# Seven-product projections joined to the feed-forward stage before them: combinations formed in its last down-projection, all three value projections as doubles by way of DRAM

## The chip, the core and the metric

The kernel runs on one core of a Trainium2 chip. The metric is device time of one execution in microseconds (us). The core has five engines that run at the same time, each in its own fixed order of instructions: TensorE (PE, matrix products), VectorE (DVE), ScalarE (ACT), GpSimd (POOL) and SyncE (SP), which only issues transfers here. Transfers (DMAs) go through queues: q1 holds those that SP issues, q0 those that POOL issues.

## What is computed

One encoder layer for 512 tokens of 1024 channels, in float32:

```
x = x + 1/2 * SwiGLU_1(RMSNorm(x))          # 1024 -> 2816 -> 1024
h = RMSNorm(x)
A, B, gates = h @ w_in                      # 4608 + 1536 + 2048 columns
  A: 3 groups of 8 heads of 64, dilated windows (128,1) (512,4) (2048,16), relative bias,
     groups combined by their softmax denominators
  B: grouped-query attention, 8 heads of 128, 2 key/value heads, normed and rotated q, k
mix = (sigmoid(gA) * (oA @ P_A) + sigmoid(gB) * (oB @ P_B)) @ w_out
x = x + mix
x = x + 1/2 * SwiGLU_2(RMSNorm(x))
y = RMSNorm(x)
```

The change lies in the projections of branch A: its q and k (24 blocks of 128 columns) and its three values V0, V1, V2 (512 columns each, one for each group).

## The kernel before

**Products.** x is held transposed, as eight tiles of 128 channels by 512 tokens. Every float32 product is made of three matmuls of rounded operands (`mm3`, L249 to L252): each operand is split into a high part H (a cast on ACT) and a rest L (a subtraction on DVE). The normed input is `hH`, `hL` (`norm_h`, L389 and L390), without the factor 1/rms of each token, which is applied to the results: `r` holds it by token in partitions, `R` by token in columns, `acc` first the sum of squares (`norm_sq`, L400, on POOL for all but the last two tiles) and later `R` in the order of residues mod 4. Weights come as tiles of 128x1024 in rings of buffers (`wr`, `wa`, `ws`, `wt`) and are split the same way (`wh` L235, `wl` L236).

**Doubles.** In parts of the kernel two blocks of 128 columns are computed together from seven half-size products instead of eight (`strassen`). Its steps are A11, S1, S2, A12, S3, S4 and A22; each is 24 matmuls of 256 columns. They need combinations of the quarters of the input (`Traw`, split into `TQ`), combinations of the weights (formed by an adding transfer on POOL, L217, and a DVE addition, L234), and additions of the results (`evict`). For the mixer this is done in `project_qk` for ten q/k pairs (f = 0, 2, ..., 8) and for V0 (f = 10). The q/k results go through `qo` to DRAM (`qk_d`, L744) and come back for attention (`fetch`, L682).

**The stages around the joint.** `ffn` ends the first feed-forward stage with its last down-projection: eight rows of matmuls, whose results are added to x (`down`, `add`, L521 and L522) and turned into hH and hL. Then the pools of the stage close. `project_qk` opens its own, and starts with a stream of plain projections: V1 token by token (`token`), then gates 0 to 3 (`feat`). While these run, the statistics r and R are made (`stat_r` L414, `stat_R` L422, `stat_p` L431), and `tq_steps` makes the combinations (L697 to L706). Then come the doubles. V1 and V0 stay in SBUF. V2 is a plain token projection too, the first item of the fill after the doubles.

**Attention A and fill.** After the doubles, `fetch` brings q and k. The remaining plain projections are fill: a generator whose groups of three matmuls (one item of `feat` is eight groups) are put between the parts of attention. First come `GAP_F` = 16 groups, then for each pair of heads `hp` scores (`scores_a`: S L831, bias tiles W by SP L804 and L805, exponentials, an exchange of maxima and sums by way of DRAM L852 to L859) and values (`values_a`: transposes T, copies PT L902, products with V L882). After the first scores, `until(fill, ("v", 2))` runs the fill until V2 is complete.

**What sets the order.** PE runs in the order in which the program is written (`manual_schedule`). On the other engines a scheduler decides the order when the kernel is built. Transfers of one queue start in that order.

Of the kernel before, what the change touches and what calls it, by code (L numbers as in the profile page):

```python
# [11 lines left out]
F32 = mybir.dt.float32  # L12
# [11 lines left out]
NSQ = 10  # L24
STEPS = ("A11", "S1", "S2", "A12", "S3", "S4", "A22")
GAP_F = 16
# [44 lines left out]
class Layer:  # L71
    def __init__(self, ctx, tc, a):
# [26 lines left out]
        self.qk_d = self.dram.tile([2 * NSQ, 128, T], F32, name="qk_d")  # L99
        gates = lambda lo, hi: [("g", j) for j in range(lo, hi)]  # L100
# [3 lines left out]
        span = {"v": ("wav", 4), "qk": ("waq", 2), "g": ("wg", 1), "b": ("wb", 4), "pa": ("wpa", 4)}  # L104
        self.order = self.ffn_order("a")
        for kind, n in self.items:
            if kind == "sw":
                self.order += [("swq", at) for at in self.slots(range(0, NSQ + 2, 2))]
# [18 lines left out]
    @staticmethod  # L127
    def slots(fs):
        at = {7 * i + 2 * j: (f, step) for i, f in enumerate(fs) for j, step in enumerate(STEPS)}
        return [at[k] for k in sorted(at)]  # L130
# [58 lines left out]
    def load(self, n):  # L189
# [17 lines left out]
        def part(q):  # L207
            if name[2] == "q" and f == NSQ:
                return self.a["wav0"][2 * int(q[1]) + int(q[2]) - 3].rearrange("p (a c) -> p a c", a=2)
            i, c = 2 * f + int(q[1]) - 1, 512 * (int(q[2]) - 1)  # L210
            return w[i:i + 3:2, :, c:c + 512].rearrange("a p c -> p a c")
# [90 lines left out]
    def strassen(self, s, fs, evict):  # L302
        st, order = {}, self.slots(fs)
        end = self.used + len(order) - 1
        for f, step in order:
# [7 lines left out]
            for j in range(2):  # L313
                for k in range(4):
                    ops = self.right(step, k)
                    if s == "q" and f == NSQ:
# [7 lines left out]
    def right(self, step, k):  # L324
# [4 lines left out]
        if self.TQ:  # L329
            c = {"S1": 0, "S3": 1, "A22": 2, "S2": 3}[step]  # L330
            return tuple(t[:, k, c, :] for t in self.TQ)
        c = {"S1": 0, "A22": 1, "S2": 2}[step]
        return self.TH[:, c, k, :], self.TL[:, c, k, :]

    def t_steps(self, g, gp):
# [4 lines left out]
        def put(d):  # L340
            if d == 0:
                both.extend(gp.tile([128, 2048], F32, tag=f"g{2 + c}", name=f"T{c}") for c in range(2))
                raw.extend(both[c // 2][:, 1024 * (c % 2):1024 * (c % 2) + 1024] for c in range(4))
            nc.scalar.activation(both[d // 4].rearrange("p (a c) -> p a c", a=2)[:, :, 256 * (d % 4):256 * (d % 4) + 256],
# [47 lines left out]
    def norm_sq(self, d, pool=NK - 2):  # L392
# [3 lines left out]
        else:  # L396
            sq = self.tmp.tile([128, T], F32, tag="t", name="sq")
            nc.scalar.activation(sq, self.x[d], AF.Square)
            eng = nc.vector if d >= pool else nc.gpsimd
# [26 lines left out]
    def stat_p(self):  # L426
        nc = self.nc
        nc.vector.tensor_copy(self.acc.rearrange("p (r m) -> p r m", r=4), self.R.rearrange("p (m r) -> p r m", r=4))
        pr = self.aux("rps")
        for r in range(4):  # L430
            nc.tensor.transpose(pr[:, r:r + 1], self.acc[0:1, 128 * r:128 * r + 128], self.ident[0:1, 0:1])  # L431
        nc.vector.tensor_copy(self.r[:, 4:8], pr[:, 0:4])

    def ffn(self, s, gin, gnext, hooks, out=None, side=None):
        with ExitStack() as ctx:
# [6 lines left out]
            self.ffn_run(s, gin, gnext, hooks, out, side or {}, pool("g", bufs=1))  # L442
            self.wx = None

    def ffn_run(self, s, gin, gnext, hooks, out, side, gp):
        nc = self.nc
        g, t, c, half = [], {}, {}, []

        def new():
            both = gp.tile([128, 2048], F32R, tag=f"g{len(g) // 2}", name="gg")  # L450
            return both[:, :1024], both[:, 1024:]
# [93 lines left out]
        for gi, hi in enumerate(ends):  # L545
            last = hi == NF
# [10 lines left out]
            rows = [(list(g), lambda ps, d=d: done(d, ps)) for d in range(NK)]  # L557
# [71 lines left out]
    def stream(self, items):  # L629
        nc = self.nc  # L630
        for kind, n in items:
            if kind == "v":
                toks = [(lambda t, r=r: t[:, r:T:4]) if n else (lambda t, r=r: t[:, 128 * r:128 * r + 128]) for r in range(4)]

                def done(j, b, g=n):
                    rc = self.r[:, j + (4 if g else 0):j + (5 if g else 1)]
                    if j % 2:
                        nc.vector.tensor_scalar(self.V[g][:, j, :], b, rc, None, op0=ALU.mult)
                    else:
                        nc.scalar.activation(self.V[g][:, j, :], b, AF.Copy, scale=rc)  # L640

                yield from self.token("wav", 4 * n, toks, done)
            elif kind == "qk":
# [10 lines left out]
            elif kind == "g":  # L654
# [6 lines left out]
                yield from self.feat("wg", n, done)  # L661
# [22 lines left out]
    def tq_steps(self, cp):  # L684
        nc = self.nc
        raw = {}

        def put(k):
            raw[k] = cp.tile([128, 4, 256], F32, tag="c1", name="Traw")
            for e in range(2):  # L690
                d = k + 4 * e
                nc.scalar.activation(raw[k][:, 2 * e:2 * e + 2], self.x[d].rearrange("p (a n) -> p a n", a=2), AF.Copy,
                                     scale=self.par[:, G_MIX + d:G_MIX + d + 1])

        def sums(k):
            b = [raw[k][:, c] for c in range(4)]
# [6 lines left out]
        def part(k):  # L703
            H, L = (t[:, k] for t in self.TQ)
            nc.scalar.copy(H, raw[k])
            nc.vector.tensor_sub(L, raw[k], f32(H))  # L706

        return [lambda fn=fn, k=k: fn(k) for k in range(4) for fn in (put, sums, part)]

    def project_qk(self):  # L710
        nc, tc = self.nc, self.tc
        with ExitStack() as ctx:
            pool = lambda n, **k: ctx.enter_context(tc.tile_pool(name=n, reuse_waits="tile", **k))
            tp = self.shifted(pool("qT", bufs=1), 64)
            self.TQ = [tp.tile([128, 4, 4, 256], F32R, name=f"TQ{c}") for c in "HL"]
            self.wx = self.shifted(pool("wxq", bufs=1), 64)
            cp, qp = pool("cq", bufs=2), pool("qo", bufs=2)
            steps = self.tq_steps(cp)
            hooks = {7: self.stat_r, 12: self.stat_R, 17: self.stat_p}
            for n, _ in enumerate(self.stream(self.items[:self.head])):  # L720
                if n in hooks:
                    hooks[n]()
                if n > 8 and n % 4 == 0 and steps:
                    steps.pop(0)()
            assert not steps
            c = {}
# [19 lines left out]
            def tokens(src, half, cols, neg):  # L746
                for j in range(2):
                    i = 2 * half + j
                    out, part, rc = self.V[0][:, i, cols], src[:, 256 * j:256 * j + 256], self.r[:, i:i + 1]
                    if neg:  # L750
                        nc.vector.tensor_scalar(out, part, rc, -1.0, op0=ALU.mult, op1=ALU.mult)
                    else:
                        nc.scalar.activation(out, part, AF.Copy, scale=rc)

            def evict(f, step, ps):
# [15 lines left out]
                elif step == "S4":  # L771
                    nc.vector.tensor_add(hi, ps, hi)
                    if f == NSQ:
                        tokens(lo, 0, slice(0, 256), False)
                        tokens(hi, 1, slice(0, 256), False)
                        return
                    o = qp.tile([128, 1024], F32, tag="qo", name="qo")
# [3 lines left out]
                elif f == NSQ:  # L781
# [484 lines left out]
```

## Time and profile before

| | us |
|---|---|
| median of 3 runs | 1260.6 (1260.19 to 1260.75) |
| the profiled execution | 1261.44 |
| its span | 1259.7 |
| ACT busy | 595.7 |
| POOL busy | 120.9 |
| last down-projection of the first stage | 314.82 to 347.49 |
| V1, then gates 0 to 3 | 347.49 to 372.29 to 394.07 |
| doubles of the mixer | 394.07 to 509.29 |
| first scores | 520.86 |

Times inside the kernel are microseconds from the start of the span. Instructions appear with the line of the kernel, their output and input names (`mm`: a PSUM bank, `gg`: the activations of the feed-forward stage) and their shape.

### The profile page before, as it was taken

The page shows a single profiled execution, that of the slowest core. Times are in us where ns is not written, and L with a number is a line of the kernel's source. Part 1 is how long each engine was busy: PE and PEld are TensorE (multiplying, and loading weights), DVE is VectorE, ACT ScalarE, POOL GpSimd, SP SyncE. Part 2 cuts the span into 40 slices and gives each one's busy share as a digit, 9 for nine tenths or more (in the row PEclk, how much of TensorE's full clock was granted, in tenths as well). Part 3 has the DMA queues.
Part 4 walks back from the last instruction along what each step waited for, and adds up shares of the span by engine and source line. Part 5 has one row for each costly group of instructions (what it writes and reads, how often), then busy time and mean ns, then how long its engine had stood idle before and what let it go on. Part 6 is the DMA issues. An engine that isn't in the chain of part 4 may idle for free.

```text
span 1259.7 us, 20123 instructions
## 1 busy us (share of the span) xinstructions
PE 1245.0 (99%) x8074; PEld 1112.1 (88%) x8074; DVE 897.4 (71%) x1349; ACT 595.7 (47%) x883; POOL 120.9 (10%) x126
## 2 busy tenths in 40 slices
PE   8999999999999999999999999999999999999997
PEld 6897999899899999977788878888889989988996
DVE  7784688478784887467746798866678747875775
ACT  8551355145453444544423456655375425532553
POOL 1111101000210110200000110000301000100001
PEclk9999999999999999999999999999999999999998
DMA  8875777242485872653223220147737536744222
GB/s 286 237 193 168 191 196 193 98 104 68 136 223 179 234 226 107 221 149 102 78 100 114 84 93 17 34 150 225 226 101 189 163 101 184 191 145 117 58 78 67
DMA packets 85981, 183.49 MB, mean 146 GB/s; under 512 B 12528, under 2 KB 19072, under 8 KB 85888
## 3 DMA queue, kind: packets, MB, share of 16 engines
q1 hardware_dynamic: 68048, 141.27, 33.4%
q0 software_dynamic: 17120, 40.39, 16.0%
q8 instruction: 63, 1.03, 0.4%
q10 hardware_dynamic: 720, 0.55, 0.1%
q14 instruction: 30, 0.25, 0.1%
HBM read 170.55 MB, written 15.29 MB: 148 GB/s over the span
## 4 chain that ended last, share of the span: by engine, by line
PE 94%; DVE 2%; DMA 2%; issue 1%; SPq 1%; ACT 0%; POOLq 0%; POOL 0%; DVEq 0%
PE mm L250 24%; PE mm L252 23%; PE mm L251 23%; PE Y L250 4%; PE Y L251 4%; PE Y L252 4%; PE X L250 2%; PE X L251 2%; PE X L252 2%; PE mm L882 1%; PE Tb L1021 1%; PE S L831 1%; PE T L900 1%; DMA d<-SO 1%; PE Sb L252 1%
## 5 line engine op out<-in xcount | busy, mean ns | idle before, releaser
L235 ACT CAST wh<-wr 128x1024 fp32r<-128x1024 f32 x139 | 145.7, 1049 | 191.2 <-PE mm L251 127.4
L250 PE MATMUL mm<-hH,wh 128*128 128x256 f32 (+1 forms) x600 | 199.8, 333 | 0.4 <-ACT hH L389 0.3
L236 DVE TENSOR_TENSOR wl<-wr,wh 128x1024 fp32r<-128x1024 f32 x139 | 169.8, 1222 | 40.9 <-ACT wh L235 40.4
L252 PE MATMUL mm<-hH,wl 128*128 128x256 f32 (+1 forms) x600 | 195.4, 326 | 0.9 <-DVE wl L236 0.9
L251 PE MATMUL mm<-hL,wh 128*128 128x256 f32 (+1 forms) x600 | 195.4, 326 | 0.6 <-DVE hL L390 0.6
L250 PE MATMUL mm<-gg,wh 128*128 128x512 f32 (+1 forms) x376 | 141.5, 376 | 0.0
L251 PE MATMUL mm<-gg,wh 128*128 128x512 f32 (+1 forms) x376 | 141.0, 375 | 0.0
L252 PE MATMUL mm<-gg,wl 128*128 128x512 f32 (+1 forms) x376 | 141.0, 375 | 0.0
L250 PEld LDWEIGHTS mm<-hH,wh 128*128 128x128 f32 x600 | 112.7, 188 | 14.8 <-issue 3.2
L252 PEld LDWEIGHTS mm<-hH,wl 128*128 128x128 f32 x600 | 112.6, 188 | 11.8 <-DVE wl L236 1.3
L251 PEld LDWEIGHTS mm<-hL,wh 128*128 128x128 f32 x600 | 112.9, 188 | 10.4 <-DVE hL L390 1.4
L235 ACT CAST wh<-wa 128x1024 fp32r<-128x1024 f32 x50 | 52.6, 1051 | 102.5 <-PE mm L251 55.4
L521 DVE TENSOR_TENSOR u<-mm,R 128x512 f32<-128x512 f32 (+1 forms) x52 | 33.8, 650 | 80.9 <-PE mm L252 80.6
L235 ACT CAST wh<-wt 128x1024 fp32r<-128x1024 f32 x50 | 52.6, 1052 | 70.3 <-PE mm L251 45.9
L236 DVE TENSOR_TENSOR wl<-wt,wh 128x1024 fp32r<-128x1024 f32 x50 | 61.2, 1224 | 33.1 <-ACT wh L235 32.2
L235 ACT CAST wh<-ws 128x1024 fp32r<-128x1024 f32 x50 | 52.6, 1052 | 67.0 <-PE mm L251 48.0
L250 PE MATMUL mm<-TH,wh 128*128 128x256 f32 x304 | 83.9, 276 | 0.0
L251 PE MATMUL mm<-TL,wh 128*128 128x256 f32 x304 | 83.9, 276 | 0.0
L252 PE MATMUL mm<-TH,wl 128*128 128x256 f32 x304 | 83.9, 276 | 0.0
L250 PEld LDWEIGHTS mm<-gg,wh 128*128 128x128 f32 x376 | 70.6, 188 | 14.0 <-PE mm L252 0.9
L252 PEld LDWEIGHTS mm<-gg,wl 128*128 128x128 f32 x376 | 70.6, 188 | 12.9
L251 PEld LDWEIGHTS mm<-gg,wh 128*128 128x128 f32 x376 | 70.6, 188 | 12.5
(262 smaller groups left out, 3212.2 us busy)
## 6 DMA issues: line engine op xcount, KB each, us to landing
wr<-in_w2a SPq DMA_DIRECT2D x22, 512.0 KB, 3.3
wr<-in_w2b SPq DMA_DIRECT2D x22, 512.0 KB, 3.4
wt<-in_w13b SPq DMA_DIRECT2D x20, 512.0 KB, 3.5
wa<-in_w13b SPq DMA_DIRECT2D x20, 512.0 KB, 3.3
wt<-in_w13b POOLq DMA_DIRECT2D x20, 512.0 KB, 5.9
wt<-in_w13a SPq DMA_DIRECT2D x18, 512.0 KB, 3.5
wt<-in_w13a POOLq DMA_DIRECT2D x18, 512.0 KB, 6.4
wa<-in_w13a SPq DMA_DIRECT2D x18, 512.0 KB, 3.3
```

The lines of the kernel that those rows point to most:

```text
L235: self.nc.scalar.copy(H, raw)
L236: self.nc.vector.tensor_sub(L, raw, f32(H))
L250: mm(out, lH, rH, start=start, stop=False, skip_group_check=more)
L251: mm(out, lH, rL, start=False, stop=False, skip_group_check=more)
L252: mm(out, lL, rH, start=False, stop=stop, skip_group_check=more)
L521: nc.vector.tensor_mul(u, ps, R)
L831: nc.tensor.matmul(*args, start=True, stop=True)
L882: nc.tensor.matmul(oc, v, p, start=st, stop=sp)
L900: nc.tensor.transpose(ps[:, 128 * b:128 * b + 128], P[h][:, c0 + 128 * b:c0 + 128 * b + 128], self.ident)
L1021: nc.tensor.transpose(pt[:, 128 * j:128 * j + 128], P[h, j][:, 128 * k:128 * k + 128], self.ident)
```

## The change

The doubles now run inside `ffn`, before its pools close (`then=self.project_qk`). The last down-projection computes its rows in the order `ROWS`, and after each of its last four rows one combination is formed from tiles k and k + 4, into the buffers TH and TL that the feed-forward stage used and a tile of its own. Of the plain projections only gate 0 is left ahead of the doubles, and its result waits in its bank until R is there. In the first double the step A12 comes second. There are eight doubles: five for q/k and three for V0, V1, V2. The results of the V doubles go to DRAM (`v_d`) and come back all three (`fetch_v`). The gates' and the fill's order, `GAP_F` and the layout of some weights follow. The four transposes of `stat_p` are gone.

```diff
+NSW = NSQ + 6
+ROWS = (0, 4, 1, 5, 2, 6, 3, 7)
-GAP_F = 16
+GAP_F = 8
...
-        self.items = ([("v", 1)] + gates(0, 4) + [("sw", 0), ("v", 2)] + gates(4, 6) + [("qk", f) for f in range(NSQ, 12)]
-                      + gates(6, 13) + [("b", g) for g in range(3)] + gates(13, 16) + [("pa", 0)])
+        self.items = (gates(0, 1) + [("sw", 0)] + gates(1, 5) + [("qk", f) for f in range(NSQ, 12)]
+                      + gates(5, 12) + [("b", g) for g in range(3)] + gates(12, 16) + [("pa", 0)])
...
+        if ahead:
+            at[1] = at.pop(6)
...
-    def norm_sq(self, d, pool=NK - 2):
+    def norm_sq(self, d, pool=tuple(range(NK))):
...
-            eng = nc.vector if d >= pool else nc.gpsimd
+            eng = nc.vector if d in pool[NK - 2:] else nc.gpsimd
...
-        pr = self.aux("rps")
-        for r in range(4):
-            nc.tensor.transpose(pr[:, r:r + 1], self.acc[0:1, 128 * r:128 * r + 128], self.ident[0:1, 0:1])
-        nc.vector.tensor_copy(self.r[:, 4:8], pr[:, 0:4])
...
             self.ffn_run(s, gin, gnext, hooks, out, side or {}, gp)
+            if then:
+                then(gp)
...
-                self.norm_sq(d)
+                self.norm_sq(d, ROWS)
+                if d >= NK // 2:
+                    if self.TQ is None:
+                        self.tq_open(gp)
+                    for step in self.tq_steps(d - NK // 2):
+                        step()
...
+    def fetch_v(self):
+        for g in range(3):
+            rows = self.v_d[g].rearrange("(m r) f -> m r f", r=4) if g else self.v_d[g].rearrange("(i p) f -> p i f", p=128)
+            self.nc.gpsimd.dma_start(self.V[g], rows)
+
+    def tq_open(self, gp):
+        q = self.g_tile(gp, 3, "TQ", F32R)
+        late = [q[:, 16 + 1024 * c:1040 + 1024 * c].rearrange("p (k n) -> p k n", k=4) for c in range(2)]
+        self.TQ = {step: (self.TH[:, c], self.TL[:, c]) for c, step in enumerate(("S1", "A22", "S2"))}
+        self.TQ["S3"] = tuple(late)
...
+        def part():
+            for src, (H, L) in ((raw[:, 0:3], (self.TH[:, :, k], self.TL[:, :, k])), (raw[:, 3], (t[:, k] for t in self.TQ["S3"]))):
+                nc.scalar.copy(H, src)
+                nc.vector.tensor_sub(L, src, f32(H))
...
+            def store_v(f, at, o):
+                dst = self.v_d[(f - NSQ) // 2].rearrange("(i p) f -> p i f", p=128)
+                nc.gpsimd.dma_start(dst[:, :, at:at + 256], o.rearrange("p (i f) -> p i f", i=4))
...
-            for _ in self.strassen("q", range(0, NSQ + 2, 2), evict):
-                pass
-            self.wx = self.TQ = None
+            def settle():
+                self.stat_R()
+                for fn, ps in held:
+                    fn(ps)
+
+            hooks = {0: self.stat_r, 1: settle, 3: self.stat_p}
+            for n, _ in enumerate(self.strassen("q", range(0, NSW, 2), evict)):
+                if n in hooks:
+                    hooks[n]()
+            self.TQ = None
...
-        self.project_qk()
...
                 self.fetch(0)
+                self.fetch_v()
...
-                    if hp == 0:
-                        self.until(fill, ("v", 2))
```

What POOL issues from the last results of the doubles to the fetches for attention, before (L744 stores q/k results, L682 fetches q and k):

```order
L744 DMA qk_d<-qo 128x2x512 [waits DMASW2_49,DVE_49]
L682 DMA qk<-qk_d 128x512 [waits DMASW3_49,PE_49]
L682 DMA qk<-qk_d 128x512 [waits DMASW6_49,DMASW4_49,Activation_49]
L682 DMA qk<-qk_d 128x512 [waits DMASW5_49]
L682 DMA qk<-qk_d 128x512
```

and in the changed kernel, at the same place (L762 stores V results, L690 fetches V0, V1 and V2, which are the tiles numbered 5404, 5405 and 5420; L685 fetches q and k):

```order
L762 DMA v_d<-qo 128x4x256 [waits DMASW3_49,Activation_49]
L690 DMA V_5404<-v_d 128x4x512 [waits DMASW4_49,DMASW7_49,DMASW0_49,PE_49]
L762 DMA v_d<-qo 128x4x256 [waits DMASW5_49,DVE_49]
L690 DMA V_5405<-v_d 128x2048 [waits DMASW6_49,DMASW2_49,DMASW1_49]
L685 DMA qk<-qk_d 128x512 [waits DMAHW2_49,DMAHW4_49,DMAHW1_49,DMAHW0_49]
L685 DMA qk<-qk_d 128x512 x3
L685 DMA qk<-qk_d 128x512 [waits DMASW3_49]
L685 DMA qk<-qk_d 128x512 [waits DMASW4_49]
L690 DMA V_5420<-v_d 128x2048 [waits DMAHW5_49,DMASW5_49]
```

Two fetches of V and the last store of a V result now stand ahead of the first fetch of q and k, and the fetch of V2 behind the sixth.

What DVE does for the last rows of the last down-projection, before (u and x: a row's result added to x; hL: the rest of the normed input; wl: a weight tile's rest; Traw: sums of a combination):

```order
L521 TENSOR_TENSOR u<-mm,R 128x512
L522 SCALAR_TENSOR_TENSOR x_81<-u,x_81 128x512
L236 TENSOR_TENSOR wl<-wr,wh 128x1024
L698 TENSOR_TENSOR Traw<-Traw 128x256
L390 SCALAR_TENSOR_TENSOR hL_112<-x_81,par,hH_104 128x512
L400 TENSOR_TENSOR acc<-acc,sq 128x512
```

and in the changed kernel, where L718 is the split of a combination:

```order
L711 TENSOR_TENSOR Traw<-Traw 128x256
L530 SCALAR_TENSOR_TENSOR x_77<-u,x_77 128x512
L709 SCALAR_TENSOR_TENSOR Traw<-Traw 128x256
L718 TENSOR_TENSOR TQ<-Traw,TQ 128x256
L709 SCALAR_TENSOR_TENSOR Traw<-Traw 128x256
L399 SCALAR_TENSOR_TENSOR hL_108<-x_77,par,hH_100 128x512
L409 TENSOR_TENSOR acc<-acc,sq 128x512
L718 TENSOR_TENSOR TL<-Traw,TH 128x3x256
L529 TENSOR_TENSOR u<-mm,R 128x512
L710 TENSOR_TENSOR Traw<-Traw 128x256
L530 SCALAR_TENSOR_TENSOR x_81<-u,x_81 128x512
L242 TENSOR_TENSOR wl<-wt,wh 128x1024
```

The combinations, which stood behind the last row (x_81), now stand among the rows, with the last hL right behind the last row quoted here.

What SP issues at the start of attention, before (wr: weights; L804 and L805: bias tiles W; d: the exchange):

```order
L202 DMA wr<-in_wg 128x1024 [waits DMAHW5_49,DVE_49]
L804 DMA W<-zd 128x256 [waits DMAHW1_49,DMASW3_49]
L805 DMA W<-zd 128x2x128 [waits DMAHW2_49]
L804 DMA W<-zd 128x256 [waits DMAHW3_49,DMASW2_49]
L202 DMA wr<-in_wg 128x1024 [waits DMAHW6_49,DVE_49]
```

and in the changed kernel (L662 stores a gate; L823 and L824 are the bias tiles):

```order
L208 DMA wr<-in_waq 128x1024 [waits DMAHW6_49,DMAHW1_49,DVE_49]
L662 DMA gate_d<-z 128x512 [waits DMAHW2_49,DVE_49]
L823 DMA W<-zd 128x256 [waits DMAHW3_49,PE_49]
L824 DMA W<-zd 128x2x128
L823 DMA W<-zd 128x256
L824 DMA W<-zd 128x2x128
L208 DMA wr<-in_waq 128x1024 [waits DMAHW7_49,DVE_49]
```

The bias tiles have moved behind the store of a gate.

More of the change, by code (lines that the diff above doesn't have):

```diff
@@ L1 @@
+import itertools
 import math
@@ L555, in done @@
                     side[gi, d]()
-            rows = [(list(g), lambda ps, d=d: done(d, ps)) for d in range(NK)]
+            rows = [(list(g), lambda ps, d=d: done(d, ps)) for d in (ROWS if last and out is None else range(NK))]
             if last and out is not None:
@@ L627, in bias_spread, with stream @@
             self.nc.gpsimd.dma_start(self.zd[h], bass.AP(tensor=src.tensor, offset=src.offset, ap=[[0, 128], [1, NV]]))
-    def stream(self, items):
+    def stream(self, items, held=None):
         nc = self.nc
+        later = lambda fn: fn if held is None else lambda ps: held.append((fn, ps))
         for kind, n in items:
[L632 to L643, printed above, removed]
+            if kind == "qk":
                 hp, g = PAIRS[n]
```

128 lines of the change are left out of this document (61 added, 67 removed).

## The prediction

> **What bounds the kernel now.** I read the page first (the span, the busy time of each engine, the engines' shares of the chain that ended last), then the waits of TensorE (PE), and then the stages around the joint.
>
> ```profile
> span 1259.7 us, 20123 instructions
> ...
> PE 1245.0 (99%) x8074; PEld 1112.1 (88%) x8074; DVE 897.4 (71%) x1349; ACT 595.7 (47%) x883; POOL 120.9 (10%) x126
> ...
> PE 94%; DVE 2%; DMA 2%; issue 1%; SPq 1%; ACT 0%; POOLq 0%; POOL 0%; DVEq 0%
> ```
>
> PE works for 1245.0 of 1259.7 us, and 94% of the chain that sets the end is PE. So a microsecond of matmul that disappears is a microsecond of time, and so is every microsecond in which PE newly waits. The waits of PE, the largest first and the first one on a value that this change touches:
>
> ```profile
> PE mm L882 <- DVE PT L902: 1.8, 1, 1.8
> ...
> PE mm L251 <- DVE hL L390: 0.6, 2, 0.3
> ```
>
> There is next to nothing to win from waiting. The table by stage says the same of the joint itself (stretch and its length, then the busy time of PE, weight loads, DVE, ACT and POOL, granted clock, DMA share, GB/s):
>
> ```profile
> 314.80:347.50 32.70, 32.70 (x147) 27.10 (x146) 24.87 (x31) 15.07 (x22) 8.45 (x6) 1.00 0.43 135
> 347.50:372.70 25.20, 25.20 (x115) 24.73 (x115) 22.42 (x36) 17.21 (x23) 4.81 (x4) 1.00 0.81 223
> 372.70:394.00 21.30, 21.30 (x95) 17.62 (x95) 8.69 (x10) 3.99 (x4) 0.00 (x0) 1.00 0.60 184
> 394.00:509.80 115.80, 115.80 (x1012) 115.76 (x1011) 90.33 (x98) 53.82 (x64) 16.63 (x19) 1.00 0.65 185
> ```
>
> These are the last down-projection of the first feed-forward stage, the token projection V1, the first gates, and the doubles (a product of two 128-column pairs done in seven half-size products). PE is busy in all of each, at full clock. **There is no gap at the joint that joining the stages could close.** The gain can come only from less matmul work; everything else the change can do to the time is a new wait, or the end of the old 1.8 us one.
>
> **Term 1, the matmul work.** V1 as a token projection starts and ends at these rows of PE's timeline; the chain view shows what else PE did in it (start, us, what):
>
> ```profile
> 347.49 0.40 PE L250 MATMUL mm<-wh,hH 128*128 128x512 f32 x1
> ...
> 372.29 0.39 PE L250 MATMUL mm<-hH,wh 128*128 128x512 f32 x1
> ```
>
> ```profile
> 353.29 0.79 PE stat L414 x8
> 354.08 0.47 PE mm L250
> 354.55 0.23 PE mm L251
> ...
> 357.83 0.44 PE rb L422 x4
> ...
> 361.92 0.34 PE rps L431 x4
> ```
>
> 24.80 us in all, less 0.79, 0.44 and 0.34 for the statistics and some 0.2 of restart behind each (0.47 where 0.23 is usual), leaves 22.6 for 96 matmuls. V2, of the same form, is spread as fill through attention and is taken at the same 22.6. The V0 double, seven of the ten last steps of the doubles, gives the price of the new form:
>
> ```profile
> 481.33 0.28 PE L250 MATMUL mm<-wh,hH 128*128 128x256 f32 x1
> ...
> 509.29 0.52 PE L250 MATMUL mm<-wh,hH 128*128 128x512 f32 x1
> ```
>
> 27.96 us for ten steps is 2.80 a step, 19.6 for a double. Two token projections for two doubles: 2 x (19.6 - 22.6) = -6.0. The four small transposes of L431 and their restart go too: -0.5. Gates and the last two q/k products are moved, not changed. **Term 1: -6.5 us.**
>
> **Term 2, the last down-projection.** The combinations for the doubles were made while V1 and gates 0 to 3 ran. Now most of them stand among the eight row results, and only gate 0 is left ahead of the doubles. VectorE's (DVE) groups in that stretch, and rows of the combinations from behind it (first and third quoted in its timeline form):
>
> ```profile
> L522 DVE SCALAR_TENSOR_TENSOR x<-u,x 128x512 f32<-128x512 f32 x8 | 6.1, 777 | 0.2
> L521 DVE TENSOR_TENSOR u<-mm,R 128x512 f32<-128x512 f32 x8 | 5.5, 690 | 1.8 <-PE mm L252 1.7
> L390 DVE SCALAR_TENSOR_TENSOR hL<-x,par,hH 128x512 fp32r<-128x512 f32 x7 | 5.2, 750 | 3.0 <-ACT hH L389 3.0
> L236 DVE TENSOR_TENSOR wl<-wr,wh 128x1024 fp32r<-128x1024 f32 x4 | 5.2, 1298 | 3.1 <-ACT wh L235 3.1
> ...
> L697 DVE SCALAR_TENSOR_TENSOR Traw<-Traw 128x256 f32<-128x256 f32 x2 | 0.8, 420 | 0.0
> ```
>
> ```profile
> 350.50 0.74 DVE L390 SCALAR_TENSOR_TENSOR hL<-x,par,hH 128x512 fp32r<-128x512 f32 x1
> ...
> 356.12 2.35 DVE L706 TENSOR_TENSOR TQL<-Traw,TQH 128x1024 fp32r<-128x1024 f32 x2
> ```
>
> One combination is 4 x 0.42 for the sums and about 1.2 for the split (2.35 for two of 1024 columns): 2.9 us. Three of the four fall inside the stretch: 24.87 + 3 x 2.9 = 33.6 us of work in 32.7, with a slow-down beside GpSimd's additions on top (one wl beside such an addition took 1.52 where 1.22 is usual):
>
> ```profile
> 327.00 1.33 POOL L400 TENSOR_TENSOR acc<-acc,sq 128x512 f32<-128x512 f32 x1 [56.36 <-ACT sq L398]
> ...
> 327.89 1.52 DVE L236 TENSOR_TENSOR wl<-wr,wh 128x1024 fp32r<-128x1024 f32 x1
> ```
>
> So DVE ends the stretch behind, by 1 to 4 us. Before, the last hL was done at 351.24, 3.75 us after the down-projection's end at 347.49, and V1 first asked for the other rows. Now gate 0 asks for it in its eighth group: a gate is 24 of V1's 96 matmuls at 22.6/96, so that is 7/8 of 5.6, 4.9 us after the end. A backlog of 2.8 us, in the middle, puts hL at 6.5: PE waits 1.6 us. With no backlog it waits nothing, with 4 us 2.9. **Term 2: +1.6 (0 to 2.9).** The Trainium skill, "GPSIMD Engine Reference", section "1. Specifications", says that GpSimd shares its SBUF interfaces with VectorE, with contention when a DVE instruction has two SBUF inputs; the 1.52 against 1.22 agrees. By that rule alone, five or six such overlaps of 0.3 us make up about half of this backlog.
>
> **Term 3, the start of attention.** Today V0 and V1 are in SBUF already, and the GpSimd queue q0 fetches q and k as soon as the last double ends (t0 = 509.29). From then 16 groups of fill run, 11.3 us, and the first scores find everything there:
>
> ```profile
> 509.76 4.30 POOL L682 DMA_DIRECT2D qk<-qk_d  x8 [9.59 <-PE mm L252]
> ...
> qk<-qk_d POOLq DMA_DIRECT2D x1, 256.0 KB, 4.7
> W<-zd SPq DMA_DIRECT2D x2, 128.0 KB, 4.4
> ```
>
> ```profile
> 520.86 1.06 PE S L831 x8
> ```
>
> In the changed order the fetch of V0 (1.05 MB), the last store of V2 (0.52) and the fetch of V1 (1.05) stand ahead of the first two q/k tiles (0.52): 3.15 MB through q0 before PE's first score. Only 8 groups of fill are ahead of it, 24 matmuls, 5.6 us. What q0 moved in two stretches, 2.5 and 2.7 us long, while it shared with q1 (packets, MB, share), and the most that all queues moved together there, 401 GB/s (last column):
>
> ```profile
> q0 software_dynamic: 193, 0.65, 67.7%
> ...
> q0 software_dynamic: 215, 0.69, 65.2%
> ```
>
> ```profile
> 518.00:520.00 2.00, 2.00 (x11) 2.00 (x10) 0.00 (x0) 0.00 (x0) 0.00 (x0) 1.00 1.06 401
> ```
>
> That is 0.26 MB/us for q0 beside other loads, and 0.40 if it had the engines alone. The first fetch took until 514.5 to land although only 0.26 MB were asked for, so I put 2.3 us of start ahead. 3.15/0.40 + 2.3 = 10.2 us after t0; 3.15/0.26 + 2.3 = 14.4. q1 still brings weights, the gate store and the bias tiles W in this time, so the shared rate is the nearer: I take 13.0. PE waits 13.0 - 5.6. **Term 3: +7.4 (4.6 to 8.8).**
>
> **Term 4, bias tiles and the second head pair.** The W tiles of the first pair stand behind the gate store on SyncE now, and those of the second behind the exchange of maxima and sums (SO), and nine groups of fill (9 x 0.7 us) between the first two score rounds are gone. One W needed long to land under load:
>
> ```profile
> W<-zd SPq DMA_DIRECT2D x1, 128.0 KB, 9.9
> ...
> 535.02 3.45 DMA d<-SO
> ```
>
> If the 3.45 us exchange and 4.4 to 9.9 us of landing are covered by term 3's wait and the first scores, this costs nothing; if the 6.3 us of lost fill covered most of it, 2.5. **Term 4: +1.0 (0 to 2.5)**, nearer the free end because the first scores wait for q and k anyway.
>
> **Term 5, the old wait.** PE's 1.76 us wait at 569.94 stood behind a late exchange:
>
> ```profile
> 563.98 0.18 DVE L861 TENSOR_TENSOR MN<-SO 128x16 f32<-128x16 f32 x1 [5.03 <-DMA SO<-d]
> ...
> 569.94 0.44 PE L882 MATMUL mm<-PT,V 128*64 128x128 f32 x4 [1.76 <-DVE PT L902]
> ```
>
> When scores start later against the fill, DVE's queue there is another one; I take the wait as gone, 2.0 with its restart. **Term 5: -2.0 (-2.0 to 0).**
>
> **Sum:** -6.5 + 1.6 + 7.4 + 1.0 - 2.0 = +1.5 us against the profiled execution, 1261.44 us (span 1259.7). The median of the runs, 1260.6, lies 0.84 lower, so the forecast is 1260.6 + 1.5 = **1262.1 us**.
>
> **Rivals.**
>
> Rival A, the loads keep up, faster. q0 gets nearly all of the 401 GB/s because most weights for the fill are already in SBUF: scores at t0 + 10.2, a wait of 4.6. With term 2 at 0.5 and term 4 at 0: -6.5 + 0.5 + 4.6 - 2.0 = -3.4, 1257.2 us. For it speaks that DMA at 512 to 520 was at its limit with 1 MB of weights that can move; against it, q0's 0.26 whenever q1 had work. The Trainium skill, "DMA: Bandwidth & Descriptors", section "Anatomy of one DMA — SWDGE (gpsimd) path", gives 2.0 us plus bytes over 436 GB/s; as an estimate 3.15 MB are then there 9.2 us after t0, a wait of 3.6 and a sum of -2.3 with my other terms. The same page, "Queues, rings and completion order", says that the engines take turns between queues packet by packet; by that rule q0 does not get all, and the trace agrees with its 0.26 beside q1.
>
> Rival B, DVE's backlog, slower. Its place is gate 0, its price one for one from the point at which the last hL is over 4.9 us behind the end of the down-projection. If waits for ScalarE's casts (3.0 us idle before hL in the rows above) are not filled by combinations, the backlog is 6 us, not 2.8: term 2 is 4.9, and the time 1262.1 + 3.3 = 1265.4 us. Against it: DVE has such idle time, and combinations can fill it.
>
> That joining does nothing by itself is no rival but my reading above: PE had no gap there.
>
> **How the numbers follow.** Forecast 0.55 (its own range 1258 to 1266 by terms 2 to 5), rival A 0.25, rival B 0.20. A measurement of this kernel can tell about 0.2%, 2.5 us: faster means below 1258.1, slower above 1263.1. The forecast's case gives faster 0.03, same 0.33, slower 0.19; A 0.22 and 0.03; B 0.02 same and 0.18 slower. Together 0.25, 0.38, 0.37. The range of 1256.5 to 1267 leaves out half of A's lower side and the end of B.
>
> **What would show it.** Steps of 2.8 us in all three V doubles and some 6 us less PE work (term 1). A wait of PE on DVE hL inside gate 0 (term 2; none, or over 4 us, speaks for A or B). A wait of the first S on the q/k fetch, with S at t0 + 13 (term 3; S at t0 + 10 is A). A wait of P on W in the first two head pairs (term 4), and no 1.8 us wait on PT (term 5). The forecast is wrong above all if q0 moves its 3.15 MB at another rate than the 0.26 to 0.40 that the rows bound, or if DVE's extra work in the down-projection fits into its idle time.

## The result and the profile after

The changed kernel takes 1275.59 us (median of 4 runs, 1272.24 to 1276.51) against 1260.67 before (4 runs): a ratio of 1.0111, 95% interval 1.009 to 1.0132. It is slower, above the range of 1256.5 to 1267. The profiled execution is the shortest of the four, 1272.24 us with a span of 1270.5: 10.8 us more than that of before (1261.44). What made the other three some 3 us longer cannot be seen in their records, except that their mean granted clock is 0.989 to 0.990, against 0.992 in the profiled one.

The page, and PE's waits, largest first (us in total, times, longest; MX, the maxima, is VectorE's last step on a tile of scores, after it has added the bias tile W):

```profile
span 1270.5 us, 20497 instructions
...
PE 1242.5 (98%) x8214; PEld 1107.6 (87%) x8214; DVE 917.2 (72%) x1372; ACT 605.3 (48%) x903; POOL 131.2 (10%) x139
...
PE 91%; DVE 4%; DMA 2%; issue 1%; ACT 1%; SPq 0%; POOL 0%; POOLq 0%; DVEq 0%
```

```profile
PE S L850 <- DMA qk<-qk_d: 11.4, 1, 11.4
PE mm L256 <- ACT hH L398: 1.9, 2, 1.0
PE S L850 <- DVE MX L855: 1.6, 2, 1.4
PE warm L1156 <- POOL R L98: 1.3, 1, 1.3
PE rb L431 <- POOL r L416: 1.0, 1, 1.0
PE mm L257 <- DVE hL L399: 1.0, 2, 0.5
```

PE's busy time fell, but by 2.5 us only, and its share of the chain went from 94% to 91%. Three new waits head the list: the first scores on the fetch of q and k, gate 0 on hH and hL, and the scores of the second head pair. The wait on PT has gone.

The stretches from the last double on (us, then busy time of PE, weight loads, DVE, ACT, POOL, granted clock, DMA share, GB/s) show a second loss that no list of waits has:

```profile
511.63:516.50 4.87, 4.87 (x24) 4.02 (x23) 2.10 (x3) 1.05 (x1) 4.03 (x8) 1.00 0.79 254
516.50:519.00 2.50, 0.76 (x4) 0.30 (x2) 1.50 (x2) 1.04 (x1) 1.03 (x2) 1.00 1.02 287
519.00:521.50 2.50, 0.00 (x0) 0.00 (x0) 0.42 (x1) 0.00 (x0) 0.00 (x0) 1.00 1.00 391
521.50:524.00 2.50, 0.00 (x0) 0.00 (x0) 0.00 (x0) 0.00 (x0) 0.54 (x1) 0.64 1.05 431
524.00:528.64 4.64, 0.00 (x0) 0.03 (x1) 0.00 (x0) 0.00 (x0) 1.61 (x3) 0.50 1.03 392
528.64:532.50 3.86, 3.86 (x12) 2.73 (x13) 1.11 (x5) 0.00 (x0) 0.54 (x1) 0.51 1.05 402
532.50:545.00 12.50, 12.50 (x92) 8.33 (x91) 7.08 (x34) 10.31 (x34) 3.19 (x6) 1.00 0.78 249
549.50:552.50 3.00, 3.00 (x9) 1.96 (x8) 1.98 (x12) 3.00 (x15) 0.00 (x0) 0.50 0.20 70
```

PE stands still from 517.3 on. Some 5 us later its granted clock falls to half, and it stays there for 3.9 us after PE has work again at 528.64. From 519 on the DMA share is 1.0, at 390 to 430 GB/s. Behind the second wait the clock is at half again for 3 us; a matmul step of 512 columns then takes 0.43 us from start to start instead of 0.23:

```profile
550.10 0.63 PE L257 MATMUL mm<-hL,wh 128*128 128x512 f32 x1
...
550.52 0.63 PE L258 MATMUL mm<-hH,wl 128*128 128x512 f32 x1
```

Behind the first wait the half clock cost about 1.9 us (3.86 us at 0.51; the eight score matmuls alone took 2.08 us where 1.06 was usual), behind the second 1.5 (3.00 us at 0.50).

### The profile page after: what moved, and what is told of

Read it like the earlier page. It is cut to its first block, busy times and chain, and to the rows that moved or that the text cites. A ratio compares the mean times of both kernels' runs of the same rounds, so it can differ in the third digit from the quotient of the medians.

```text
span 1270.5 us, 20497 instructions
## 1 busy us (share of the span) xinstructions
PE 1242.5 (98%) x8214; PEld 1107.6 (87%) x8214; DVE 917.2 (72%) x1372; ACT 605.3 (48%) x903; POOL 131.2 (10%) x139
## 3 DMA queue, kind: packets, MB, share of 16 engines
q8 instruction: 64, 1.05, 0.3%
## 4 chain that ended last, share of the span: by engine, by line
PE 91%; DVE 4%; DMA 2%; issue 1%; ACT 1%; SPq 0%; POOL 0%; POOLq 0%; DVEq 0%
PE mm L256 23%; PE mm L257 22%; PE mm L258 22%; PE Y L257 4%; PE Y L256 4%; PE Y L258 4%; PE X L256 2%; PE X L257 2%; PE X L258 2%; PE S L850 1%; PE mm L901 1%; DMA qk<-qk_d 1%; PE Tb L1040 1%; PE T L919 1%; DVE wl L242 1%
## 5 line engine op out<-in xcount | busy, mean ns | idle before, releaser
L241 ACT CAST wh<-wr 128x1024 fp32r<-128x1024 f32 x133 | 139.4, 1049 | 178.4 <-PE mm L257 126.5
L242 DVE TENSOR_TENSOR wl<-wr,wh 128x1024 fp32r<-128x1024 f32 x133 | 163.0, 1226 | 29.3 <-ACT wh L241 28.9
L257 PE MATMUL mm<-TL,wh 128*128 128x256 f32 x384 | 106.0, 276 | 0.0
L258 PE MATMUL mm<-TH,wl 128*128 128x256 f32 x384 | 106.0, 276 | 0.0
L256 PE MATMUL mm<-TH,wh 128*128 128x256 f32 x384 | 106.0, 276 | 0.0
L241 ACT CAST wh<-wa 128x1024 fp32r<-128x1024 f32 x54 | 56.8, 1051 | 96.0 <-PE mm L257 48.3
L241 ACT CAST wh<-ws 128x1024 fp32r<-128x1024 f32 x54 | 56.8, 1052 | 76.6 <-PE mm L257 49.2
L242 DVE TENSOR_TENSOR wl<-wt,wh 128x1024 fp32r<-128x1024 f32 x54 | 66.1, 1224 | 34.5 <-ACT wh L241 33.6
L242 DVE TENSOR_TENSOR wl<-wa,wh 128x1024 fp32r<-128x1024 f32 x54 | 67.0, 1241 | 27.5 <-ACT wh L241 27.5
L256 PEld LDWEIGHTS mm<-gg,wh 128*128 128x128 f32 x376 | 70.6, 188 | 14.1 <-PE mm L258 0.9
```

Of the source, the lines that this page charges most:

```text
L241: self.nc.scalar.copy(H, raw)
L242: self.nc.vector.tensor_sub(L, raw, f32(H))
L256: mm(out, lH, rH, start=start, stop=False, skip_group_check=more)
L257: mm(out, lH, rL, start=False, stop=False, skip_group_check=more)
L258: mm(out, lL, rH, start=False, stop=stop, skip_group_check=more)
```

## The experiments

The first theory was that of the prediction with a larger size: the fetches of V in q0, ahead of q and k, make the wait, and the waits with their clock drops are the loss. Its rivals: the shorter fill, the work of VectorE in the front, or the volume of transfers whatever their order. Times are medians; before is 1260.5 to 1260.7 in each session.

**e1, V behind q and k** (`tail` is the last fetch of q and k).

```diff
-            self.nc.gpsimd.dma_start(self.V[g], rows)
+            with self.tc.issue_after(self.tail.ins):
+                self.nc.gpsimd.dma_start(self.V[g], rows)
```

> The changed kernel with one edit: GpSimd issues the fetches of V0, V1 and V2 behind the six fetches of q and k. Theory 1 (place in the queue): only the stores (about 1.05 MB) and the first two q/k tiles (0.52 MB) go ahead of the first scores at 0.25 MB/us, so these start about 8 us after the last double instead of 17.0, PE waits 0 to 3 us instead of 11.4, and the kernel takes 9 to 13 us less than the changed one. Rival (all transfers after the doubles share the DMA engines, whatever their order): the wait stays above 8 us and the kernel gains less than 4 us. Values need V0 some 60 us after the last double, so no theory expects a new wait on V.

**e2, longer fill.** GAP_F = 16.

> The changed kernel with GAP_F back at 16. Both theories: 8 more groups of fill, 5.5 us, run inside the wait of 11.4 us, so about 5.9 us of it are left. If idle time beyond about 5.6 us is what lowers PE's granted clock, the drop to 0.50 disappears or gets short, and the kernel gains 6.5 to 7.5 us; if the clock does not depend on the length of the wait, it gains 5.5. If the wait grew by the added weight loads, it gains less than 4.

**e3, PE kept busy.**

```diff
                 gap(GAP_F)
+                warm = self.bank()
+                for _ in range(50):
+                    nc.tensor.matmul(warm, self.hH[0][:, :128], self.hH[0], start=True, stop=True)
```

> The changed kernel with 50 matmuls of 512 columns, 11.4 us, whose result nobody reads, between the 8 groups of fill and the first scores. PE is busy but does nothing more. Theory 1: scores start at the same time (17 us after the last double) at full clock, and the kernel gains the 1.9 us that the half clock cost behind the wait. Rival (the clock falls for another reason, or costs nothing): the granted clock still drops and the time is the changed kernel's within 0.5 us.

**e4, the last combinations later** (`hpin` is the last hL).

```diff
-                if d >= NK // 2:
+                if d in (4, 5):
...
+                elif d == 7:
+                    with self.tc.issue_after(self.hpin.ins):
+                        for step in self.tq_steps(2) + self.tq_steps(3):
+                            step()
```

> The changed kernel with the last two of the four combinations queued on VectorE behind the last hL of the down-projection. If the combinations among the rows make the 2.9 us of waits in gate 0, these fall below 0.5 us, gate 0 takes 5.5 to 6 us instead of 9.5, and the kernel gains 3 to 4 us, less what S1 of the first double waits for the late combinations (0 to 1.5 us). Rival (VectorE has too much to do there in any order): S1 waits about as long as gate 0 did before, and the gain is below 1 us.

Measured: e1 1274.04 us, e2 1274.57, e3 1275.94, e4 1275.07. No edit gained over 1.6 us against 1275.59. Yet each did what it was made for. PE's waits in e1, e2 and e3:

```profile
PE S L851 <- DMA qk<-qk_d: 6.9, 2, 4.2
PE mm L902 <- DVE PT L922: 2.9, 1, 2.9
```

```profile
PE S L850 <- DMA qk<-qk_d: 6.6, 1, 6.6
PE S L850 <- DVE MX L855: 5.4, 2, 5.2
```

```profile
PE S L850 <- DVE MX L855: 5.1, 1, 5.1
```

In e1 the first wait fell to 4.2 us, but 2.7 came up at the q and k of the second pair and 2.9 at PT. In e2 it fell to 6.6, but the second pair waited 5.2. In e3 there was no idle time and no clock drop at the first scores, but 5.1 at the second pair. In e4 the front's waits fell from 2.9 to 1.2 us, and 1.8 us came up at r, whose first step stood behind the late combinations. So the point at which PE stands still does not set the pace there: what PE wins at one point it waits for at the next. Theory 1 in its simple form falls; in these runs the place in the queue decided only where the wait stood.

The next theory was that PE's fill is too short for what the transfers need from the last double to the second pair (the cover theory).

**e5, the fill of before.** GAP_F = 16, more gates ahead of q/k pairs 10 and 11 in the fill, and

```diff
+                    if hp == 0:
+                        gap(8)
                     if held:
```

> The changed kernel with the fill of before at the start of attention: GAP_F 16, and 8 groups between the first two score rounds (before had 8 there by the wait for V2), paid for by gates taken from later fill. After the first four runs the theory is now: from the last double to the second head pair the transfers set the pace, and each microsecond of fill that PE lacks there is a wait (cover theory). It expects 6 us of wait at the first scores, at most 1 us at the second head pair, the clock drop of the second pair gone, and 1263 to 1267 us. Rival (the bias tiles and the exchange are late by themselves because q0 is full of V): the wait of the second pair stays at 3 us or more, and the time above 1270 us.

**e6, before with the short fill.** GAP_F = 8 in the kernel before.

> The kernel before with only GAP_F changed from 16 to 8, the change's number. V0 and V1 are in SBUF there, so q0 carries only q and k. If the V round trip makes the late q and k, the first tiles land 5 us after the last double, just as the fill ends: wait below 1 us, no clock drop, 1260 to 1263 us. If the shorter fill alone were enough for the loss, the first scores would wait more than 3 us and the time were above 1266 us.

**e7, two gates in turn.**

```diff
+            for i, k in enumerate(ROWS):
+                s = slice(128 * k, 128 * k + 128)
+                for (H, L), ps in zip(ws, banks):
+                    self.mm3(ps, H[:, s], L[:, s], self.hH[k], self.hL[k], i == 0, i == NK - 1)
```

> The changed kernel with gates 0 and 1 together ahead of the doubles, in turn, and each in the order of ROWS, so that the last two rows are asked for 8.2 and 9.5 us after the down-projection instead of 2 and 4.8. Both waits of gate 0, 2.9 us with 0.9 of restart, go; there is one gate less of fill later. If the front's waits count in full, the time is 1271 to 1273 us (3 to 4 us less than the changed kernel); if the transfers behind the doubles take the gain back, it stays above 1274.

**e8, together.** The edits of e7, the 8 groups of e5, and V fetched behind the q and k of the second pair.

> Together: the two gates in turn ahead of the doubles, the fetches of V behind the q/k tiles of the second head pair, and 8 groups of fill between the first two score rounds (GAP_F stays 8). Cover theory: the first scores wait 2 to 4 us, the second pair and its q and k at most 1, values none; 1259 to 1264 us. Rival (the round trip of V costs its transfer time wherever it stands): a new wait of 5 us or more on V or on the exchange, above 1268 us.

Measured: e5 1274.38 us, e6 1260.58 (0.9999 of before, 0.999 to 1.0009), e7 1273.7, e8 1274.86. The short fill alone does nothing: e6's first scores waited 1.4 us on q and k, and its time is that of before. The cover theory falls too: with all the fill, e5 waits 6.8 us at the first scores and 3.5 later. e7 took PE's waits in gate 0 away (1.1 us is left at r), but of some 3.8 us its median shows 1.9, and its runs (1272.5 to 1275.2) lie within those of the changed kernel. e8's waits of PE, then what SyncE waited for, show where its gain went:

```profile
PE S L863 <- DVE MX L868: 6.6, 3, 5.1
PE S L863 <- DMA qk<-qk_d: 4.0, 1, 4.0
```

```profile
SPq L888 <- DMA d<-SO: 9.9, 2, 7.1
```

The fetches of V are out of the way of the first q and k now, and collide with the exchange of the first pair instead. Landing times of two of its stores (KB, us from issue), in e8 and before:

```profile
d<-SO SPq DMA_DIRECT2D x2, 1.0 KB, 6.8
```

```profile
d<-SO SPq DMA_DIRECT2D x2, 1.0 KB, 2.2
```

A store of 1 KB needs 6.8 us where it needed 2.2. Next to it in SyncE's queue stand the bias tiles of the second pair, and the scores wait for those.

The third theory is the volume of transfers. The stores of V1 and V2 and the three fetches come to 5.2 MB; 4.2 of them (both stores of V2's halves, 1.05 MB, and the fetches) move behind the last double. The DMA share there reached 1.06 before the change already (518 to 520 us).

**e9, bias tiles early,** loaded one head pair ahead.

```diff
-            w = ap.tile([128, T], F32, tag="W", name="W", bufs=2)
+            w = self.ap.tile([128, T], F32, tag="W", name="W", bufs=4)
```

> The changed kernel with four buffers for the bias tiles instead of two, and each pair's tiles loaded a pair ahead, so that those of the second head pair no longer stand in SyncE's queue behind the exchange of the first. If that place in the queue makes the second pair's wait (1.6 us in the profiled execution of the changed kernel, 5 in those of its variants) with the clock drop behind it, the wait falls below 1 us and the kernel gains 3 to 5 us: 1270 to 1273 us. If the transfers as a whole set the pace, the exchange (values wait) takes its place: above 1274.

**e10, all of it.** e8 and e9 together.

> All edits of e8 and the early bias tiles of e9 together. If each wait is one place in a queue, none above 3 us is left and the time is 1260 to 1265 us. If the volume of transfers sets the pace, a wait of 4 us or more comes up behind the exchange or at values, and the time stays above 1269.

**e11, no way through DRAM.** Stores of V1 and V2 and all fetches are left out, and VectorE fills the three V tiles with 1.0, so that the layer's result is not the right one.

```diff
-            self.nc.gpsimd.dma_start(self.V[g], rows)
+            self.nc.vector.memset(self.V[g], 1.0)
...
+                if f == NSQ:
+                    nc.gpsimd.dma_start(dst[:, :, at:at + 256], o.rearrange("p (i f) -> p i f", i=4))
```

> The changed kernel without the way of V through DRAM: the stores of V1 and V2 and the three fetches are left out, and VectorE sets the three V tiles to 1.0, so that the products with V use those numbers. All else, the short fill and SyncE's queue too, is as changed. If the V transfers are the loss, the first scores wait less than 1 us, the second pair less than 2, no clock drop is left, and the time is 1255 to 1261 us. If the shorter fill, the front or the order on SyncE made it, the time stays above 1266 us.

**e12, that traffic in the kernel before,** with each fetch of q and k issued behind it.

```diff
+                src = self.a["w13b"]
+                nc.gpsimd.dma_start(self.V[2].rearrange("p (a i) f -> p a (i f)", a=2), src[0:2].rearrange("a p c -> p a c"))
+                for n in range(2):
+                    dum = ap.tile([128, NP], F32, tag="P", name="P", bufs=4)
+                    self.tail = nc.gpsimd.dma_start(dum.rearrange("p (a c) -> p a c", a=2),
+                                                    src[2 * n + 2:2 * n + 4, :, 0:960].rearrange("a p c -> p a c"))
                 self.fetch(0)
```

> The kernel before with 3.0 MB of loads that nobody uses (into V2's tile ahead of its writing, and into two free tiles of P) ahead of the q/k fetches in q0: about what V adds to that queue in the changed kernel. If this traffic is the loss, the first scores come about 16 to 17 us after the last double against 11.3 us of fill, wait 5 us, the exchange gets slower, and the time is 1266 to 1273 us. If it is not, it stays within 1 us of before.

Measured: e9 1276.43 us, e10 1274.75, e11 1261.48, e12 1267.3 (1.0048 of before, 1.0031 to 1.0065). No move has gained more than 1.9 us. In e9 the wait of the second pair went, and 2.9 us came up at the values; in e10 the waits stand at the exchange (10.1 us, on DVE L905) and at q and k (4.4). **Taking V's way through DRAM away gains 14.1 us, nearly all of the loss, with the front, the short fill and SyncE's order as changed.** Putting 3.0 MB of such traffic into the kernel before costs 6.6 us. At the 0.39 MB/us of its full stretch these are 7.7 us of DMA time. They stand ahead of q and k, so that e12 shows the cost and does not separate volume from place. PE's waits of e12, and its stretch of standing still with the half clock behind it:

```profile
PE S L832 <- DMA qk<-qk_d: 4.9, 1, 4.9
PE mm L883 <- DVE PT L903: 1.1, 1, 1.1
```

```profile
520.00:525.50 5.50, 0.61 (x5) 0.33 (x3) 1.23 (x1) 2.33 (x2) 1.61 (x3) 0.85 1.02 391
525.50:531.00 5.50, 5.50 (x18) 3.51 (x18) 1.64 (x9) 1.79 (x7) 0.00 (x0) 0.53 1.00 383
```

Two orders that keep V's traffic were not run, and the traces leave room for both. In e11 q and k are issued from 507.49 on, 5.1 us before the last double ends; in the changed kernel they come 3.2 us behind its end, after V2's stores. All eight of e11 land within 6.3 us and the first scores do not wait, although its DMA share behind the last double is 0.99. So e11 changes the place of q and k too. And V could be fetched behind the first exchange: in the changed kernel the DMA share is 0.14 from 550 to 555 and 0.46 from 555 to 560, and the first product with V starts at 565.05. That V's way makes the loss is shown. That its volume does so in any order is not; it holds for the orders that were run.

This left the question why e11, with some 7 us less matmul work, is no faster than before. Its waits, and the stretch behind the first of them:

```profile
PE S L851 <- DVE MX L856: 2.4, 1, 2.4
PE mm L256 <- ACT hH L398: 1.9, 2, 1.0
PE mm L257 <- DVE hL L399: 0.9, 2, 0.5
```

```profile
536.80:543.50 6.70, 6.60 (x36) 5.30 (x36) 4.13 (x24) 4.73 (x20) 0.00 (x0) 0.51 0.43 123
```

A wait of 2.4 us on late bias tiles was followed by 6.7 us at half clock, worth 3.3; and the front's 2.8 us of waits (3.8 with restarts) are there as in the changed kernel. Part of the first may be the experiment's own: the three fills of V with 1.0, 1.76 us each, hold VectorE from 514.04 to 520.08, and the chain that leads to the late scores at 536.90 runs through them. How much they cost is not shown.

**e13, V1 as a double, its transfers inside.** The kernel before with one more double, the first, for V1:

```diff
+FQ = (12, 0, 2, 4, 6, 8, 10)
...
+                if at:
+                    nc.gpsimd.dma_start(self.V[(f - NSQ) // 2], self.v_d[(f - NSQ) // 2].rearrange("(m r) f -> m r f", r=4))
```

> The kernel before with V1 alone as a double, the first of the seven: its results go to DRAM and come back to V1's tile while the other six doubles run, so that no V transfer falls behind the last double. Gates 0 to 4 stand ahead of the doubles, V2 stays fill, GAP_X is 3. If a V double really saves 3.0 us of PE and the loss comes only from transfers behind the last double, the time is 1257 to 1258.5 us, with the first scores on time. If a V double saves nothing, or its store and fetch hurt anywhere, it is 1260 us or more.

**e14, e11 with the two waits taken away.** e11, e7 and e9 together.

> The changed kernel without the way of V through DRAM (as in e11, V tiles set to 1.0), with the two gates in turn ahead of the doubles (e7) and the bias tiles loaded a pair ahead (e9). If the 3.8 us of waits in gate 0 and the 2.4 us wait with the clock drop (some 3.5 us) at the second head pair are what ate the 6.5 us of matmul work in e11, the time is 1252 to 1255 us. If they are only where PE happens to wait, it stays above 1258.

**e15, e13 with the gate given back to the fill.**

```diff
-        self.items = (gates(0, 5) + [("sw", 0), ("v", 2)] + gates(5, 7) + [("qk", f) for f in range(NSQ, 12)]
+        self.items = (gates(0, 4) + [("sw", 0), ("v", 2)] + gates(4, 7) + [("qk", f) for f in range(NSQ, 12)]
```

> As e13, with four gates ahead of the doubles instead of five, so that the fill of attention is as long as before (GAP_X 4 again), and the combinations formed one step every second group. In e13's trace waits of 1.6 and 1.4 us stood where fill ran out (after the last values of branch A, and in branch B); if missing fill made them, they fall below 0.5 us and the time is 1257 to 1259 us, faster than before by 2 to 3 us. If the saving of the V double is given back elsewhere, it stays at 1260 or above, with a new wait of some 2 us in the first double for the combinations.

Measured: e13 1260.78 us (1.0002 of before, 0.9993 to 1.0011), e14 1258.3 (0.9981, 0.9972 to 0.999), e15 1260.83 (1.0003, 0.9994 to 1.0012). e14, which leaves V's way out and can't be used, is faster than before by 2.4 us; the two edits were worth 3.2 us against e11, where I expected 6.5 to 9.5. In the place of the two waits stand 2.2 us on the values of the first pair, with 3 us of reduced clock, and 1.4 us where fill has run out. e13 has no traffic of V behind the last double, and PE's busy time fell by 2.6 us, near the 3.0 of term 1; its time did not. Waits of PE in e13, then in e15:

```profile
PE mm L254 <- DVE oL L954: 1.4, 1, 1.4
PE Tb L1050 <- DVE Pb L1044: 1.2, 1, 1.2
```

```profile
PE mm L911 <- DVE PT L931: 2.6, 1, 2.6
PE Tb L1050 <- DVE Pb L1044: 1.3, 1, 1.3
```

In e15 the wait of 1.4 went with the gate given back; that of branch B stayed, so my reason for it was wrong. The wait of 2.6 us on PT is from the longest of its eleven runs, 1263.05 us. What holds the last 2 us of a V double back is open. No version that computes the layer was faster than the kernel before.

## Why the prediction was wrong, point by point

Against the profiled execution, by the steps of the sum:

| term | forecast | measured | how |
|---|---|---|---|
| 1, matmul work | -6.5 | -7.2 | 46.58 us of V1 and four gates and 22.6 of V2 went; 40.15 of doubles, gate 0's own 5.45 and three later gates (16.34) came |
| 2, the front | +1.6 | +4.0 | gate 0 takes 9.49 us instead of 5.45 |
| 3, first scores | +7.4 | +11.5 | the wait of 11.4 and the restart |
| 4, second pair | +1.0 | +1.8 | 1.6 and the restart |
| 5, the old wait | -2.0 | -2.0 | it has gone |
| PE's clock | none | +3.4 | 1.9 and 1.5 behind two waits |
| start of the kernel | none | -0.7 | the down-projection starts at 314.11, not 314.82 |

This sums to 10.8, as the spans differ. The waits came where the prediction put them, and term 1, against which all is set, was near. **Two steps failed: term 3 had too little volume ahead of q and k, and there was no term for the clock.**

Term 3 took 3.15 MB and 13.0 us, and it was 17.0. The landings (KB, us from issue) of the fetch of V0, issued at 512.09, and of the first q/k fetch, issued at 514.85, and then what q0 moved from 513.93 to the first scores at 528.64 (packets, MB, share):

```profile
V<-v_d POOLq DMA_DIRECT2D x1, 1024.0 KB, 10.3
```

```profile
qk<-qk_d POOLq DMA_DIRECT2D x1, 256.0 KB, 12.9
```

```profile
q0 software_dynamic: 1030, 4.25, 73.6%
```

Up to 513.93 q0 moved nothing, so the start of 2.3 us behind t0 = 511.63 came out. It then moved 4.25 MB in 14.7 us, which is 0.29 MB/us. The sum had the same rate inside (3.15 MB in 13.0 us less 2.3), taken between 0.26 and 0.40 for no reason of this stretch; that it fits is luck. At that rate 4.25 MB and the start make 16.8 us: **the term of the sum that was mis-sized is the 3.15 MB.** Two things were missing. The store of V2's first half, 0.52 MB, was left out: it was issued at 511.20, and none of it had moved at t0. And q0 did not finish the first two tiles of q and k before it began what was issued behind them: 4.25 less 3.67 MB, some 0.6, belong to later transfers.

The row that I quoted there (401 GB/s, DMA share 1.06) also said that the engines had no room, so that a megabyte put there costs its time. As an estimate, 4.2 MB at 0.4 MB/us are 10.5 us. The nine versions of the changed kernel that kept these megabytes at the start of attention, e1 to e5 and e7 to e10, all stayed 13 to 16 us above before. I had made the place in the queue the matter, where the volume at the start of attention was.

The clock stood nowhere in the sum: "everything else the change can do to the time is a new wait, or the end of the old 1.8 us one" leaves no room for matmuls that run slower behind a wait. The Trainium skill, "TensorE: Matmul & The Clock Gate", "Part 1: The HAM clock gate", says that PE runs at half clock after an idle window of some 3.4 us and until about as long a busy one has passed, and reports a fall 5.2 us after the last matmul. The trace agrees for the first wait: some 5 us until the fall, 3.9 until the return. Term 3 itself allowed waits of 4.6 to 8.8 us, so by that rule a fall of the clock belonged into the sum. For the second wait it does not agree: 1.4 us of waiting, broken by a few matmuls, were enough.

Term 2: the last hL was done at 355.63, 8.9 us after the down-projection's end at 346.77, where 6.5 was forecast. This is the last of the rows' hL in DVE's timeline, with the row result ahead of it:

```profile
352.22 0.68 DVE L529 TENSOR_TENSOR u<-mm,R 128x512 f32<-128x512 f32 x1
...
354.89 0.74 DVE L399 SCALAR_TENSOR_TENSOR hL<-x,par,hH 128x512 fp32r<-128x512 f32 x1
```

PE was done with the last row at about 347, but DVE, which runs in order, came to it at 352.22: the rest of the row before it and its combination stood ahead. I had taken only a mean backlog. I also missed that gate 0 asks for row 3, the seventh in ROWS, in its fourth group: half of the 2.9 us are waits there. Rival B named this mechanism with a price of 4.9 us; 4.0 came.

Term 4 came out near its size in this execution, and where it was put: ahead of that wait VectorE stood 3.7 us for a bias tile W. In e2, e3 and e4 the same wait was 4.8 to 5.4 us. That it is this which makes three of the four runs 3 us longer is likely and not shown. Rival A (the loads keep up, 0.40 MB/us) is refuted by the 0.29 above.

## What to carry to other kernels

Before moving results through memory to save matrix work, look at the DMA share of the stretch in which they return. Where it is near 1 and PE is about to wait for other transfers of that stretch, count the bytes over the full rate as time, count all that is issued close together, and do not trust a better place within the stretch to hide them. An operand that needs another layout is better fetched while PE has long work that waits for no transfer (e13's V1 went at a DMA share of 0.72 to 1.04 and made PE wait nowhere there), which must be weighed against the memory that it holds. Where PE waits more than a few microseconds, add what the lower clock behind the wait costs; and where an in-order engine gets more work among the rows of a stage, ask what stands ahead of the last row, not how full the engine is on average.

## What the hardware showed that I had not expected

A wait of 2.4 us (e11) was followed by 6.7 us at a granted clock of 0.51, while waits of 1.4 us (e6) and 1.76 us (before) left it at 1.00. The length of one wait alone does not decide it. A transfer of 1 KB took 6.8 us to land beside a full q0 (e8), three times the 2.2 us of before. Fetches that GpSimd issued close together shared q0: some 0.6 MB of later ones moved before the first two tiles of q and k had landed.
